# A second pair of up-projection columns by seven block products, and the last down-projection part in the common order of work

## The chip, the cores and the metric

One core of a Trainium2 chip runs the kernel as one launch. The metric is the device time of the launch in microseconds (us). Of the engines, PE is the matrix engine, DVE the vector engine, ACT the scalar engine, POOL and SP the two that here mainly issue DMAs. Each works through its own queue in order. Which instruction stands where in a queue was fixed when the program was compiled.

## The reference, cut to what matters

The whole is one step of a hybrid backbone for 128 context tokens and 512 latent tokens (640 in all, `D_MODEL` 1024). The change lies in its last stage, the gated MLP with a three-tap convolution along the tokens between the up-projection and the gate:

```python
def conv_ffn(h, w_up, conv_w, conv_b, w_down):
    L = h.shape[1]
    u = h @ w_up                       # (tokens, 1024) @ (1024, 2*2816)
    up = jnp.pad(u, ((0, 0), (1, 1), (0, 0)))
    uc = conv_w[0] * up[:, :L] + conv_w[1] * up[:, 1:L + 1] + conv_w[2] * up[:, 2:L + 2] + conv_b
    a, g = jnp.split(uc, 2, axis=-1)
    return (jax.nn.silu(g) * a) @ w_down
```

Its result is scaled, added to the residual and normalised. All matrices are float32. The kernel gets float32 products out of a faster matrix format by splitting each operand in a high part (rounded) and a low part (the rest), and by three matmuls for one: high by high, high by low, low by high.

## The kernel before, in words

**Tiles.** The 2816 hidden columns are 22 tiles of 128, taken in 11 pairs `p`. Pair `p` has an a half (`i` = 0) and a g half (`i` = 1), each 256 columns of `w_up`. The activations (`h2`, high and low) stand transposed, 128 features by tokens, 8 feature tiles, and tokens in two runs of `HW` = 322 columns.

**Two ways to multiply.** `plain_group` computes one half of a pair directly: four banks (two hidden tiles by two token runs) with 24 matmuls each, 96 in all. `unit_group` sees the same product as a product of 2 by 2 blocks and computes it by seven block products (`prod(m)`, in the order 1, 5, 6, 2, 3, 7, 4) with 12 matmuls each, 84 in all. For that it needs combinations of weight blocks, which `prep(m)` forms in place in the loaded tile and splits into high and low (DVE for four additions and five subtractions, ACT for copies, for m = 2 and 3 a DMA that accumulates), and combinations of activation blocks (`sa[1]` to `sa[4]`, high and low). Product 5 reads `sa[1]`, product 6 `sa[2]`, product 3 `sa[4]`, product 7 `sa[3]`. The results go to the pair's columns with a few additions on DVE and ACT.

**The sums of activations.** `diff` and `neg_sum` (L1174 to L1181) build the combinations in two scratch tiles on DVE, 128 by 1288 elements an operation; `hi_of` (L1188, ACT) and `lo_of` (L1191, DVE) split them. The fourth, in `last_sum`, is different: its high and low part overwrite the activation block `aq[1, 0]` itself, which `plain_group` reads. So `last_sum` is called inside the last bank of the plain g half.

**The order of work.** Pair 0 is computed ahead, while the last rows are still normalised. Then `groups` lists what follows: before the change pair 1's a half plain, `d0[0]`, pair 1's g half plain, `d0[1]`, then for each further pair two unit groups, with `down_groups` (the down-projection of finished pairs, four hidden tiles at a time) in between. `seq` is the list of all items of PE; the seventh product of a unit group is held back behind two items of the next group. `pump` traces loads and preparations as early as two `raw` tiles (1 MB each) and eight `wh` tiles allow. For PE the order written is the order run. DVE, ACT, POOL and SP get their order from a planner which, at each moment of a simulated run, takes the ready instruction that was traced first.

**The end before the change.** After the loop the last part of the down-projection (hidden tiles 18 to 21) stood alone: `load_w` loaded and split its weights, with DVE subtractions for the low parts, and `last_mm` ran tiles 18 and 19 for the first four row blocks, all column halves, which fills the time in which pair 10 passes convolution and gate. Then tiles 20 and 21 follow, `down_add`, `square` and `finish`.

The lines that fix the seven products' weights and activations are

```python
        PLAN = {1: ((0, 0), None), 5: ((0, 0), (0, 1)), 6: ((0, 0), (1, 1)), 2: ((1, 0), None),
                7: ((0, 1), (1, 1)), 4: ((0, 0), (1, 0)), 3: ((1, 1), None)}
        AOP = {1: aq[0, 0], 5: sa[1], 6: sa[2], 2: aq[0, 1], 7: sa[3], 4: aq[1, 1], 3: sa[4]}
```

Of the kernel before, what the change touches and what calls it, by code (L numbers as in the profile page):

```python
# [18 lines left out]
P = 128  # L19
DM = 1024  # L20
KD = DM // P
NT = 5
# [4 lines left out]
NF = FF // P  # L27
# [41 lines left out]
def hybrid_step(ctx: ExitStack, tc: tile.TileContext, a: dict, o: dict):  # L69
# [60 lines left out]
    def load_w(src, kk, n, lo_eng=None):  # L130
        return w_split(w_raw(src, kk, n), kk, n, lo_eng)

    def w_raw(src, kk, n):
        raw = wp([P, 4 * 512], F32, tag="raw", bufs=2)
        nc.sync.dma_start(raw[:, :kk * n].rearrange("p (k n) -> p k n", n=n), src.rearrange("(k p) n -> p k n", p=P))
        return raw

    def w_split(raw, kk, n, lo_eng=None):
        hs, ls = [], []
        step = 1024 // n  # L140
        for k0 in range(0, kk, step):
            w = min(step, kk - k0) * n
            rv = raw[:, k0 * n:k0 * n + w]
            hi = wp([P, 1024], F32R, tag="wh", bufs=8)[:, :w]
            lo = wp([P, 1024], F32R, tag="wh", bufs=8)[:, :w]
            nc.scalar.copy(hi, rv)  # L146
            if lo_eng == "dma":
                nc.scalar.activation(lo, rv, AF.Copy, scale=-1.0)
                nc.gpsimd.dma_start(lo, rv, accum_op=ALU.add)
            else:  # L150
                (lo_eng or V).tensor_sub(lo, rv, hi.bitcast(F32))  # L151
            for k in range(w // n):
                hs.append(hi[:, k * n:(k + 1) * n])
                ls.append(lo[:, k * n:(k + 1) * n])
        return hs, ls

    def mm3(ps, ah, al, bh, bl, start, stop):
        nc.tensor.matmul(ps, ah, bh, start=start, stop=False)  # L158
        nc.tensor.matmul(ps, ah, bl, start=False, stop=False)  # L159
        nc.tensor.matmul(ps, al, bh, start=False, stop=stop)  # L160
# [127 lines left out]
    mm = Pool("mm1", 5, space=PSUM)  # L288
# [233 lines left out]
    for i in (1, 0):  # L522
        ct, st = ctab[i], stab[i]
# [72 lines left out]
    mm = Pool("mm2", 1, space=PSUM)  # L596
# [129 lines left out]
    mm = Pool("mm3", 5, space=PSUM)  # L726
# [118 lines left out]
    st = states()  # L845
# [168 lines left out]
    def gt_pair():  # L1014
        return [gtp([P, 2, 2 * HW], F32R, tag=f"gt{i}", bufs=2) for i in range(2)]
# [7 lines left out]
    def x_row(dtype=F32):  # L1023
        return x1p([P, 768], dtype, tag="row", bufs=4)
# [3 lines left out]
    w_out, w_up, w_down = a["w_out"][0], a["w_up"][0], a["w_down"][0]  # L1028
# [40 lines left out]
    raw = w_raw(w_up[:, :256], 8, 256)  # L1069
# [6 lines left out]
    with tc.manual_schedule(engines={ET.PE}):  # L1076
        bank = {}
# [52 lines left out]
    def conv(f, i):  # L1130
        u, q = ub[f % 2][i], i * NF + f
        v = cvs[f, i] = x_row()[:, :641]
        nc.scalar.activation(v, u[:, 1:642], AF.Identity, scale=cw[:, 1, q:q + 1], bias=cw[:, 3, q:q + 1])
        V.scalar_tensor_tensor(v, u[:, 0:641], cw[:, 0, q:q + 1], v, op0=ALU.mult, op1=ALU.add)
        V.scalar_tensor_tensor(v, u[:, 2:643], cw[:, 2, q:q + 1], v, op0=ALU.mult, op1=ALU.add)
# [3 lines left out]
    def gate(f):  # L1139
        if f // 2 not in gts:  # L1140
            gts[f // 2] = gt_pair()
        r = [x[:, f % 2, :641] for x in gts[f // 2]]
        ca, cg = cvs[f, 0], cvs[f, 1]
        tg = t7([P, 641], tag="tg", bufs=1)
        nc.scalar.activation(tg, cg, AF.Tanh, scale=0.5)
        V.scalar_tensor_tensor(cg, tg, 1.0, cg, op0=ALU.add, op1=ALU.mult)
        V.tensor_mul(ca, ca, cg)
        nc.scalar.copy(r[0], ca)
        V.tensor_sub(r[1], ca, r[0].bitcast(F32))
# [17 lines left out]
    acc = Pool("acc7", 4, space=PSUM)  # L1167
    mm = Pool("mm7", 4, space=PSUM)
# [10 lines left out]
    def neg_sum(out, x, ys):  # L1179
        V.scalar_tensor_tensor(out, x, -1.0, ys[0], op0=ALU.mult, op1=ALU.subtract)  # L1180
        V.tensor_sub(out, out, ys[1])  # L1181
# [5 lines left out]
    def hi_of(m, x):  # L1187
        nc.scalar.copy(sa[m][0], x)  # L1188

    def lo_of(m, x):  # L1190
        V.tensor_sub(sa[m][1], x, sa[m][0].bitcast(F32))  # L1191
# [11 lines left out]
    def last_sum():  # L1203
        neg_sum(xs[0], xs[1], q[0, 1])
        hi_of(4, xs[0])
        lo_of(4, xs[0])
# [4 lines left out]
    def down_mm(ps, t, fs, w, part=None):  # L1211
        c0 = 0 if t == 0 else 129 + (t - 1) * P
        for n, f in enumerate(fs):
            if part is not None and n not in part:
                continue
            g = [x[:, f % 2, c0:c0 + P] for x in gts[f // 2]]
            mm3(ps, g[0], g[1], w[0][n], w[1][n], n == 0, n == len(fs) - 1)

    def down_add(ps, t, c0):
        n = ps.shape[1]  # L1220
        gs = slice(c0, c0 + n)
        tm = x_tmp()[:, :n]
        V.tensor_mul(tm, ps, gb[:, t == 0, gs])
        V.tensor_add(x1[:, t, gs], x1[:, t, gs], tm)  # L1224
# [32 lines left out]
    later = []  # L1257

    def plain_group(p, i):
        st = {}  # L1260

        def load():
            st["raw"] = w_raw(w_up[:, i * FF + 2 * p * P:i * FF + 2 * (p + 1) * P], 8, 256)

        def prep():
            st["w"] = w_split(st["raw"], 8, 256, "dma")

        def bank(f, h):
            def go():
                up_cols(f, i, st["w"], h * HW, (h + 1) * HW)  # L1270
                if h:
                    if i and f % 2:
                        last_sum()
                    later.append(lambda: conv(f, i))
                    if i and f % 2:
                        later.append(lambda: gate(f - 1))
                        later.append(lambda: gate(f))
            return go

        items = [bank(2 * p + f, h) for f in range(2) for h in range(2)]  # L1280
        return load, [(prep, 4, items)], items
# [74 lines left out]
    def down_groups(fs, step, after=()):  # L1356
        rows = slice(fs[0] * P, (fs[-1] + 1) * P)

        def group(g):
            st = {}  # L1360

            def load():
                st["raw"] = w_raw(w_down[rows, g * 512:(g + 1) * 512], len(fs), 512)

            def prep():
                st["w"] = w_split(st["raw"], len(fs), 512, "dma")

# [12 lines left out]

    d0 = down_groups([0, 1], 0)
    groups = [plain_group(1, 0), d0[0], plain_group(1, 1), d0[1]]
    for p in range(2, NF // 2):
        groups += [unit_group(p, 0), unit_group(p, 1)]
        if p % 2:
            d = down_groups(list(range(2 * p - 4, 2 * p)), 2 if p == 9 else 1, (2 * p + 1, 2 * p))
            groups = groups[:-1] + [d[0], groups[-1], d[1]]
    seq, held = [], []
    for _, _, items in groups:
        for x in items[:-1] if len(items) == 7 else items:  # L1390
# [34 lines left out]
    for fn in later:  # L1425
        fn()

    fs = list(range(NF - 4, NF))
    rows = slice(fs[0] * P, NF * P)
    ws = [load_w(w_down[rows, g * 512:(g + 1) * 512], 4, 512) for g in range(2)]  # L1430
    fg = wp([P, 4 * 512], F32, tag="raw", bufs=2)[:, :DM]
    nc.sync.dma_start(fg, a["final_g"].unsqueeze(0).to_broadcast([P, DM]))
    cols = {t: ((0, 512), (512, 256), (768, 256)) if t == NT - 1 else ((0, 512), (512, 512)) for t in range(NT)}
    bank = {}

    def last_mm(t, c0, n, part):
        if (t, c0) not in bank:
            pool, tag = ((acc, "acc"), (mm, "mm"))[t % 2]
            bank[t, c0] = pool([P, 512], tag=tag)[:, :n]
        g, cc = c0 // 512, slice(c0 % 512, c0 % 512 + n)  # L1440
        down_mm(bank[t, c0], t, fs, [[x[:, cc] for x in y] for y in ws[g]], part)

    with tc.manual_schedule(engines={ET.DVE, ET.PE}):
        for t in range(NT - 1):
            for c0, n in cols[t]:
                last_mm(t, c0, n, (0, 1))
        for t in range(NT):
            for c0, n in cols[t]:
                last_mm(t, c0, n, (2, 3) if t < NT - 1 else (0, 1, 2, 3))
                down_add(bank[t, c0], t, c0)  # L1450
                square(t, c0, n)
                if c0 == 0 and t == 3:
                    finish(0, 3)
        finish(NT - 2, 2)
# [37 lines left out]
```

## Time and profile before

| what | us |
| --- | --- |
| time, median of 3 runs (lowest to highest) | 1202.6 (1199.58 to 1203.64) |
| time of the profiled execution | 1202.29 |
| its span, first to last instruction | 1200.5 |
| PE busy in the span | 1160.6 |
| DVE busy | 736.5 |
| ACT busy | 567.1 |

The span is 1.8 us shorter than the time of the same execution; the rest lies before the first and after the last instruction. A row of the timeline gives the start and the length of an instruction in us, its engine, its line, its operation, the tile written and the tiles read, and in brackets how long the engine had been idle and who released it. A length includes the time that an instruction spends in the engine's pipeline, so consecutive starts show the rate better than lengths. In a row of the windows view, after the bounds, each engine's busy time stands with the number of its instructions, and behind the engines the granted clock of PE (1.00 is full), the busy share of the DMA engines and GB/s.

### The profile page before, as it was taken

To read this page: it belongs to the slowest core of one execution; us is meant where nothing else is said; L and a number is where in the kernel's file an instruction comes from. 1 tells how busy PE (TensorE), PEld (TensorE's weight loads), DVE (VectorE), ACT (ScalarE), POOL (GpSimd) and SP (SyncE) were. 2 spreads that over 40 slices of the span, in tenths; PEclk is the share of its full clock that TensorE was granted. 3 is DMA by queue.
4 is the path that set the end of the run, shared out by engine and by line. 5 is a ranking of instruction groups with operands and counts; after the bars stand their busy time and mean duration, and the time that the engine had idled before them with its cause. 6 is when DMAs were issued, how large, how long until landed. Compare 5 with 4: busy or idle time off the path is not lost.

```text
span 1200.5 us, 18330 instructions
## 1 busy us (share of the span) xinstructions
PE 1160.6 (97%) x7329; PEld 1043.8 (87%) x7329; DVE 736.5 (61%) x1428; ACT 567.1 (47%) x1013; POOL 173.9 (14%) x181
## 2 busy tenths in 40 slices
PE   4999999999999999999999999999999999999994
PEld 3788899999988888889999988999899898998884
DVE  5676977763234436453323259947677597677877
ACT  4345756551132324433322236667557465574453
POOL 0032200000012100042111122011111121122102
PEclk9999999999999999999999999999999999999998
DMA  8832111115564431112122459346657556677532
GB/s 283 273 113 71 36 36 36 36 59 166 198 215 148 141 97 44 36 36 70 39 92 82 158 126 184 89 113 116 139 140 170 131 105 133 128 136 171 120 96 87
DMA packets 129509, 139.54 MB, mean 116 GB/s; under 512 B 26240, under 2 KB 96976, under 8 KB 129424
## 3 DMA queue, kind: packets, MB, share of 16 engines
q1 hardware_dynamic: 104432, 109.01, 28.1%
q0 software_dynamic: 24272, 28.05, 14.4%
q8 instruction: 57, 0.93, 0.3%
q10 hardware_dynamic: 720, 1.31, 0.3%
q14 instruction: 28, 0.23, 0.1%
HBM read 110.31 MB, written 6.03 MB: 97 GB/s over the span
## 4 chain that ended last, share of the span: by engine, by line
PE 82%; DVE 8%; ACT 3%; issue 2%; DMA 2%; POOL 1%; SPq 0%; DVEq 0%; ACTq 0%; POOLq 0%
DMA weights.wh.379_10430<-weights.raw.369_10202 1%; DVE acts.u2.2_101 L1065 1%; DVE x1.u1.1_6381 L1224 1%; DMA xin.u1.1_112<-in_x_sample 0%; DMA weights.wh.394_10721<-weights.raw.382_10453 0%; DMA weights.raw.402_10915<-in_w_down 0%; POOL f0.s.5_3525 L901 0%; DVE acts.u1.1_100 L1064 0%; DVE x1.u1.1_6381 L1037 0%; DVE x1.u1.1_6381 L1254 0%; DVE gt.gt0.5_7260 L1175 0%; PE mm1.mm.11_318 L158 0%; PE mm7.mm.46_9644 L1327 0%; PE mm7.mm.34_8912 L1327 0%; PE mm7.mm.22_8180 L1327 0%
## 5 line engine op out<-in xcount | busy, mean ns | idle before, releaser
L790 POOL TENSOR_TENSOR ret.r2k.6_3635<-ret.u5.5_3528,ret.u1.1_3521 128x256 f32<-128x256 f32 x2 | 1.4, 740 | 205.0 <-ACT ret.u5.5_3528 L786 205.0
L1251 POOL TENSOR_TENSOR x1.u1.1_6381<-x1.u1.1_6381,weights.raw.407_10925 128x512 f32<-128x512 f32 x5 | 7.5, 1502 | 39.6 <-ACT x1.tm.112_10994 L1241 28.3
L839 DVE SCALAR_TENSOR_TENSOR ret2.u1.1_4322<-ret2.u1.1_4322,const.u14.14_94 64x128 f32<-64x128 f32 x24 | 6.8, 336 | 6.6 <-ACT ret2.u1.1_4322 L832 6.5
L1338 DVE TENSOR_TENSOR t7.u4.4_6930<-t7.u4.4_6930,const.u1.1_70 128x322 f32<-128x322 f32 x9 | 4.5, 496 | 10.1 <-ACT const.u1.1_70 L1337 10.1
L524 POOL TENSOR_TENSOR p1.u1.1_618<-p1.u3.3_622,p1q.u1.1_612 128x512 f32<-128x512 f32 x1 | 1.6, 1600 | 59.5 <-DMA p1.u4.4_624<-in_cache_k 59.5
L355 PE MATMUL mm1.mm.1_180<-const.u1.1_70,xin.u1.1_112 128*128 128x128 f32 x4 | 1.1, 434 | 9.3 <-DVE xin.u1.1_112 L348 9.3
L151 DVE TENSOR_TENSOR weights.wh.183_6570<-weights.raw.181_6567,weights.wh.182_6569 128x1024 fp32r<-128x1024 f32 x1 | 1.2, 1226 | 14.3 <-ACT weights.wh.182_6569 L146 14.3
L841 DVE SCALAR_TENSOR_TENSOR ret2.u1.1_4322<-ret2.u1.1_4322,const.u14.14_94 64x128 f32<-64x128 f32 x24 | 6.6, 382 | 4.8 <-ACT ret2.u1.1_4322 L834 4.8
L792 DVE TENSOR_TENSOR ret.u5.5_3528<-ret.u5.5_3528,ret.u1.1_3521 128x512 f32<-128x512 f32 x5 | 3.5, 693 | 9.4 <-POOL ret.r2k.8_3706 L790 3.3
L355 PEld LDWEIGHTS mm1.mm.1_180<-const.u1.1_70,xin.u1.1_112 128*128 128x128 f32 x4 | 0.7, 216 | 9.5 <-DVE xin.u1.1_112 L348 9.5
L392 ACT CAST acts.u1.1_100<-f0.s.1_113 128x640 fp32r<-128x640 f32 x4 | 2.9, 729 | 12.9 <-DVE f0.s.1_113 L390 12.9
L792 DVE TENSOR_TENSOR ret.u4.4_3527<-ret.u4.4_3527,ret.u1.1_3521 128x512 f32<-128x512 f32 x5 | 3.5, 692 | 9.0 <-POOL ret.r2k.11_3886 L790 4.7
L392 ACT CAST acts.u1.1_100<-f0.s.2_114 128x640 fp32r<-128x640 f32 x4 | 2.9, 730 | 9.9 <-DVE f0.s.2_114 L390 9.9
L151 DVE TENSOR_TENSOR weights.wh.108_4352<-weights.raw.106_4349,weights.wh.107_4351 128x1024 fp32r<-128x1024 f32 x1 | 1.2, 1226 | 10.3 <-ACT weights.wh.107_4351 L146 10.3
L901 POOL TENSOR_TENSOR f0.s.5_3525<-f0.s.5_3525,ret2.ny20.11_4904 128x512 f32<-128x512 f32 x5 | 6.0, 1238 | 9.1 <-DVE ret2.ny20.11_4904 L218 9.1
L146 ACT CAST weights.wh.112_4507<-weights.raw.111_4505 128x1024 fp32r<-128x1024 f32 x1 | 1.1, 1050 | 13.3 <-PE mm3.mm.36_4220 L159 13.3
L493 ACT ACTIVATE f0.s.3_724<-f0.s.3_724,p1q.ny20.11_892 128x128 f32<-128x128 f32 x20 | 6.0, 388 | 2.5 <-DVE p1q.ny20.11_892 L216 2.5
L828 POOL DMA_DIRECT2D out_new_state_ret_fwd<-ret.r2k.25_4345 x1 | 0.7, 662 | 43.8 <-ACT ret.r2k.25_4345 L827 43.8
L258 DVE COPY mod2.wr.9_4312<-aux3.aux.15_4279 128x128 f32<-128x128 f32 x1 | 0.3, 291 | 10.9 <-PE aux3.aux.15_4279 L255 10.9
L1235 DVE TENSOR_TENSOR x1.u1.1_6381<-x1.u1.1_6381,gate.u1.1_5311 128x512 f32<-128x512 f32 x10 | 6.7, 687 | 0.0
L1338 DVE TENSOR_TENSOR t7.u3.3_6929<-t7.u3.3_6929,const.u1.1_70 128x322 f32<-128x322 f32 x9 | 4.4, 494 | 3.4 <-ACT const.u1.1_70 L1337 3.4
L146 ACT CAST weights.wh.182_6569<-weights.raw.181_6567 128x1024 fp32r<-128x1024 f32 x1 | 1.1, 1055 | 11.5 <-PE mm3.mm.83_6401 L159 11.5
(7021 smaller groups left out, 4887.1 us busy)
## 6 DMA issues: line engine op xcount, KB each, us to landing
spill.u1.1_6389<-x1.u1.1_6381 POOLq DMA_DIRECT2D x5, 512.0 KB, 4.4
xin.u1.1_112<-in_x_sample SPq DMA_DIRECT2D x4, 512.0 KB
p0.u5.5_130<-in_w_mod SPq DMA_DIRECT2D x2, 1024.0 KB
p0.u6.6_135<-in_w_mod SPq DMA_DIRECT2D x2, 1024.0 KB
p0.u7.7_138<-in_w_mod SPq DMA_DIRECT2D x2, 1024.0 KB
mod.wm.2_2921<-in_w_mod SPq DMA_DIRECT2D x1, 2048.0 KB
mod.wm.4_3072<-in_w_mod SPq DMA_DIRECT2D x1, 2048.0 KB
mod.wm.6_3227<-in_w_mod SPq DMA_DIRECT2D x1, 2048.0 KB
```

What stands on the lines that cost most here:

```text
L151: (lo_eng or V).tensor_sub(lo, rv, hi.bitcast(F32))
L392: nc.scalar.copy(hT[0][:, k, :], xk)
L493: nc.scalar.activation(x[:, j], x[:, j], AF.Copy, scale=rstd[:, j:j + 1])
L792: V.tensor_mul(z, z, r1[:, t, 0:1, :].to_broadcast([P, 8, 64]))
L839: V.scalar_tensor_tensor(Ss[0:64, hh, st + 1, j], Ss[0:64, hh, st, j], cdsel[0:64, h:h + 1], Ss[0:64, hh, st + 1, j], op0=ALU.mult, op1=AL ...
L841: V.scalar_tensor_tensor(Ss[64:128, hh, 2 - st, j], Ss[64:128, hh, 3 - st, j], cdsel[64:128, h:h + 1], Ss[64:128, hh, 2 - st, j], op0=ALU. ...
L901: nc.gpsimd.tensor_mul(ov, ov, rso[:, 4 * t:4 * t + 4].unsqueeze(2).to_broadcast([P, 4, P]))
L1065: V.tensor_sub(d[1], hm, d[0].bitcast(F32))
L1224: V.tensor_add(x1[:, t, gs], x1[:, t, gs], tm)
L1235: V.tensor_mul(x1[:, t, gs], x1[:, t, gs], gb[:, t == 0, gs])
L1251: nc.gpsimd.tensor_mul(x1[:, t, lo], x1[:, t, lo], fg[:, lo])
L1338: V.tensor_sub(u[1][:, hi_u], u[1][:, hi_u], u3[i])
```

## The change

Pair 1 goes through `unit_group` for both halves; only pair 0 is plain. `last_sum` is called before the list of groups is built. The gates of pair 1 move behind the last item of `d0[1]`. The last part of the down-projection becomes two groups, `last_group(0)` and `last_group(1)`, at the end of `groups`: their items (tiles 18 and 19 of row blocks 0, 2, 1, 3) stand in `seq`, so the seventh product of pair 10 is held back behind two of them; their loads and preparations go through `pump`, and the low parts come from ACT and an accumulating DMA, as in the other down groups, and no longer from DVE. `plain_group` stays in the file, but nothing calls it.

```diff
-                    if i and f % 2:
+                    later.append(lambda: conv(f, i))
+                    if f % 2:
                         last_sum()
-                    later.append(lambda: conv(f, i))
-                    if i and f % 2:
-                        later.append(lambda: gate(f - 1))
-                        later.append(lambda: gate(f))
...
-    d0 = down_groups([0, 1], 0)
-    groups = [plain_group(1, 0), d0[0], plain_group(1, 1), d0[1]]
+    d0 = down_groups([0, 1], 0, (3, 2))
+    last_sum()
+    groups = [unit_group(1, 0), d0[0], unit_group(1, 1), d0[1]]
...
+    def last_group(g):
+        st = {}
+
+        def load():
+            st["raw"] = w_raw(w_down[fs[0] * P:, g * 512:(g + 1) * 512], 4, 512)
+
+        def prep():
+            ws[g] = w_split(st["raw"], 4, 512, "dma")
+
+        items = [lambda t=t: last_mm(t, g * 512, 512, (0, 1)) for t in (0, 2, 1, 3)]
+        return load, [(prep, 4, items)], items
+
+    groups += [last_group(0), last_group(1)]
...
-    ws = [load_w(w_down[rows, g * 512:(g + 1) * 512], 4, 512) for g in range(2)]
...
     with tc.manual_schedule(engines={ET.DVE, ET.PE}):
-        for t in range(NT - 1):
-            for c0, n in cols[t]:
-                last_mm(t, c0, n, (0, 1))
```

`last_mm`, `cols` and `bank` are moved up and not altered.

More of the change, by code (lines that the diff above doesn't have):

```diff
@@ L1387, in hybrid_step, with last_mm @@
             groups = groups[:-1] + [d[0], groups[-1], d[1]]
+    fs = list(range(NF - 4, NF))
+    cols = {t: ((0, 512), (512, 256), (768, 256)) if t == NT - 1 else ((0, 512), (512, 512)) for t in range(NT)}
+    bank, ws = {}, {}
+    def last_mm(t, c0, n, part):
+        if (t, c0) not in bank:
+            pool, tag = ((acc, "acc"), (mm, "mm"))[t % 2]
+            bank[t, c0] = pool([P, 512], tag=tag)[:, :n]
+        g, cc = c0 // 512, slice(c0 % 512, c0 % 512 + n)
+        down_mm(bank[t, c0], t, fs, [[x[:, cc] for x in y] for y in ws[g]], part)
+    def last_group(g):
[7 more added lines that the diff above has]
+    groups += [last_group(0), last_group(1)]
     seq, held = [], []
@@ L1426, in hybrid_step @@
         fn()
-    fs = list(range(NF - 4, NF))
-    rows = slice(fs[0] * P, NF * P)
-    ws = [load_w(w_down[rows, g * 512:(g + 1) * 512], 4, 512) for g in range(2)]
     fg = wp([P, 4 * 512], F32, tag="raw", bufs=2)[:, :DM]
     nc.sync.dma_start(fg, a["final_g"].unsqueeze(0).to_broadcast([P, DM]))
[L1433 to L1441, printed above, removed]
     with tc.manual_schedule(engines={ET.DVE, ET.PE}):
-        for t in range(NT - 1):
-            for c0, n in cols[t]:
-                last_mm(t, c0, n, (0, 1))
         for t in range(NT):
```

## The prediction

> **What bounds the kernel now.** I read the page first, for the shares, then the list of waits of PE, for what PE lacks, then the timelines and windows of the two places that the change touches.
>
> ```profile
> span 1200.5 us, 18330 instructions
> PE 1160.6 (97%) x7329; PEld 1043.8 (87%) x7329; DVE 736.5 (61%) x1428; ACT 567.1 (47%) x1013; POOL 173.9 (14%) x181
> ...
> PE mm7.mm.64_10766 L1324 <- ACT const.u1.1_70 L1337: 2.1, 1, 2.1
> PE aux3.aux.99_7057 L1053 <- DVE gt.gt0.1_6395 L1044: 0.9, 1, 0.9
> PE acc7.acc.46_10513 L159 <- DMA weights.wh.379_10430<-weights.raw.369_10202: 0.8, 1, 0.8
> ```
>
> PE works 97% of the span, and in the MLP its longest wait is 2.1 us. So matmuls taken away count in full, but only where PE still finds its operands ready. DVE's 61% is an average; what matters is DVE where the second pair begins:
>
> ```profile
> 749.30:769.40 20.10, 19.91 (x125) 19.71 (x123) 19.98 (x18) 12.98 (x17) 0.85 (x1) 1.00 0.32 85
> 769.40:780.00 10.60, 10.56 (x71) 10.56 (x72) 10.53 (x13) 6.27 (x10) 0.84 (x1) 1.00 0.44 106
> ...
> 780.00:785.00 5.00, 5.00 (x32) 4.82 (x32) 0.77 (x1) 3.29 (x5) 0.56 (x1) 1.00 0.01 3
> ```
>
> The third busy time is DVE's: 19.98 of 20.10 us and 10.53 of 10.60. For 30 us around the start of pair 1 (769.4) DVE has no free time; only behind 780 it has (0.77 of 5). PE is full there too, because plain products need nothing from DVE.
>
> **The change part by part.**
>
> *Matmuls saved.* From the windows of PE alone, one plain half and one small down group:
>
> ```profile
> 769.44:783.88 14.44, 14.44 (x97) 1.00 0.33 78
> 805.16:812.14 6.98, 6.98 (x33) 1.00 0.58 65
> ...
> 1146.02 0.31 PE L1324 MATMUL mm7.mm.66_10825<-acts.u1.1_100,weights.wh.393_10703 128*128 128x322 f32 x1
> 1147.82 0.31 PE L1324 MATMUL mm7.mm.65_10780<-acts.u1.1_100,weights.wh.394_10721 128*128 128x322 f32 x1
> ```
>
> 96 matmuls (the 97th belongs to the next item) take 14.44 us, 0.150 each; a block product of 12 takes 1147.82 - 1146.02 = 1.80 us. Two halves lose 2 x (96 - 84) = 24 matmuls: **-3.6 us**.
>
> *The new wait.* Plain products read only the activations. The unit group reads `sa[1]` second, `sa[2]` third and `sa[4]` fifth. PE reaches product 1 at 769.44 (row below) and product 3 four products later, 769.4 + 4 x 1.80 = **776.6**. When is `sa[4]` there?
>
> ```profile
> 745.82 1.05 DVE L1061 TENSOR_SCALAR x1.row.56_7074<-aux3.aux.100_7069,const.u8.8_88,const.u10.10_90 128x128 f32<-128x128 f32 x3 [1.19 <-PE aux3.aux.100_7069 L1053]
> 749.30 1.49 DVE L1175 TENSOR_TENSOR gt.gt0.5_7260<-acts.u1.1_100 128x1288 f32<-128x1288 f32 x1
> 755.32 0.88 DVE L1134 SCALAR_TENSOR_TENSOR x1.row.57_7212<-t7.u1.1_6927,t7.u5.5_6935,x1.row.57_7212 128x641 f32<-128x641 f32 x1
> 768.67 1.50 DVE L1191 TENSOR_TENSOR sums.u6.6_6923<-gt.gt0.5_7260,sums.u5.5_6922 128x1288 fp32r<-128x1288 f32 x1
> 770.08 0.89 DVE L1134 SCALAR_TENSOR_TENSOR x1.row.60_7224<-t7.u4.4_6930,t7.u5.5_6935,x1.row.60_7224 128x641 f32<-128x641 f32 x1
> 776.03 1.50 DVE L1181 TENSOR_TENSOR gt.gt0.5_7260<-gt.gt0.5_7260,acts.u2.2_101 128x1288 f32<-128x1288 f32 x1
> 777.44 0.83 DVE L1147 TENSOR_TENSOR x1.row.59_7220<-x1.row.59_7220,x1.row.60_7224 128x641 f32<-128x641 f32 x1
> ...
> 769.44 0.42 PE L1123 MATMUL mm7.mm.5_7315<-acts.u1.1_100,weights.wh.199_7296 128*128 128x322 f32 x1 [0.23 <-ACT gate.u1.1_5311 L275]
> ...
> 803.94 1.27 ACT L1188 CAST acts.u1.1_100<-gt.gt0.5_7260 128x1288 fp32r<-128x1288 f32 x1
> 805.41 1.49 DVE L1191 TENSOR_TENSOR acts.u2.2_101<-gt.gt0.5_7260,acts.u1.1_100 128x1288 fp32r<-128x1288 f32 x1
> ...
> 796.35 0.69 DVE L1310 TENSOR_TENSOR weights.wh.215_7486<-weights.raw.211_7433,weights.wh.215_7486 128x512 fp32r<-128x512 f32 x1 [7.32 <-ACT weights.wh.215_7486 L1305]
> 797.07 1.42 DVE L1302 TENSOR_TENSOR weights.raw.211_7433<-weights.raw.211_7433 128x512 f32<-128x512 f32 x2
> ```
>
> The difference behind `sa[4]` is already made early: its second step starts at 776.03 and the next DVE row at 777.44. Only its split waited for the plain half (803.94). After the change the split follows at once: 1.3 us ACT, 1.4 us DVE. This alone gives 780.2. But DVE also has to prepare the unit group's weights: a subtraction for product 1, an addition and a subtraction each for 5 and 6, again for 7 and 4, nine operations of 0.6 to 0.7 us. The plain half needed none; its low parts came by DMA. The scratch tile is reused (768.67 must end before the last sum may start), so the sums can't begin sooner, and the planner prefers them and pair 0's convolutions and gates, traced earlier.
>
> Five small operations, 5 x 0.61 = 3.1 us, must stand before product 6 has run; all nine are 5.5. The 1.2 us hole before 745.82 may take two of them. DVE can fill ACT's 1.3 us with the gate operations that stood behind 777.44. Early end: 780.2 + 3.1 - 1.2 - 1.3 = 780.8. Late end: 780.2 + 5.5 = 785.7, less a little where small operations fill bubbles, 785. I take the middle, **783.0**: planning by readiness lets the small ones slip between dependent sums, but not all of them. PE then stands 783.0 - 776.6 = 6.4 us (4.2 to 8.4). If instead the weights come late, product 5 or 6 stands and product 3 doesn't; the end is DVE's total either way.
>
> *The clock after a stall.*
>
> ```profile
> 1151.40 0.40 PE L158 MATMUL acc7.acc.51_10929<-weights.wh.398_10907,gt.gt0.25_10640 128*128 128x512 f32 x1
> 1154.38 0.51 PE L1324 MATMUL mm7.mm.64_10766<-acts.u1.1_100,weights.wh.396_10759 128*128 128x322 f32 x1 [2.12 <-ACT const.u1.1_70 L1337]
> 1157.64 0.55 PE L158 MATMUL acc7.acc.51_10929<-weights.wh.398_10907,gt.gt0.25_10640 128*128 128x512 f32 x1
> ...
> 1156.00:1157.00 1.00, 1.00 (x5) 1.00 (x5) 0.34 (x1) 0.63 (x1) 0.00 (x0) 0.50 0.00 0
> 1158.00:1159.00 1.00, 1.00 (x6) 0.80 (x5) 0.65 (x2) 0.97 (x2) 0.00 (x0) 1.00 0.00 0
> ```
>
> After 2.12 us of idling the granted clock is 0.50 until about 1158: the 12 matmuls take 3.26 us, not 1.80. So a stall of this length adds 1.5 us, and I add **1.6** for the longer one. The Trainium skill, "TensorE: Matmul & The Clock Gate", section "HAM oscillation — how this bites in real kernels", says that idle gaps beyond about 3.4 us bring this on; here 2.12 us did, so the measurement decides. Head: 6.4 + 1.6 - 3.6 = **+4.4 us** (4.2 + 1.5 - 3.6 = +2.1 to 8.4 + 1.7 - 3.6 = +6.5).
>
> *What is hidden.* The weights of the g half and of `d0`: DVE has room again behind 780, and product 4 and five down items (1.8 + 7.0 = 8.8 us) lie ahead of the g half.
>
> ```profile
> 751.91 0.37 SPq L135 DMA_DIRECT2D weights.raw.203_7306<-in_w_up  x1
> ```
>
> The load of the g half went out at 751.91, when the first `raw` tile was free. That tile is now freed some 33 us later (785), as its additions are in place; SP then loads the g half into the tile of `d0[0]`. If that cover fails, a 1 MB load (5 us, below) shows. The moved gates of pair 1 are needed only by pair 3's down group and by pair 2's convolution buffers, six products (10.8 us) later. All at nothing.
>
> *The last part.* Before, PE waits for ACT, whose queue is held by a load:
>
> ```profile
> 1147.70 0.37 SPq L135 DMA_DIRECT2D weights.raw.402_10915<-in_w_down  x1
> 1144.99 1.06 ACT L146 CAST weights.wh.398_10907<-weights.raw.397_10905 128x1024 fp32r<-128x1024 f32 x1
> 1152.95 1.04 ACT L146 CAST weights.wh.403_10917<-weights.raw.402_10915 128x1024 fp32r<-128x1024 f32 x1 [4.80 <-DMA weights.raw.402_10915<-in_w_down]
> 1153.90 0.42 ACT L1337 COPY const.u1.1_70<-mm7.mm.64_10766 128x322 f32<-128x322 f32 x1
> ...
> 1166.77 0.83 DVE L1149 TENSOR_TENSOR gt.gt1.28_10892<-x1.row.108_10808,gt.gt0.27_10891 128x641 fp32r<-128x641 f32 x1 [0.80 <-ACT gt.gt0.27_10891 L1148]
> 1168.27 0.39 PE L158 MATMUL acc7.acc.51_10929<-weights.wh.400_10911,gt.gt0.27_10891 128*128 128x512 f32 x1
> ...
> weights.wh.205_7309<-weights.raw.198_7294 POOLq DMA_DIRECT2D x1, 512.0 KB, 4.5
> weights.wh.379_10430<-weights.raw.369_10202 POOLq DMA_DIRECT2D x1, 512.0 KB, 7.8
> ```
>
> Tiles 20 and 21 begin at 1168.27, as eight items and the gates (1167.6) are done. After the change two items (12 matmuls, 2.8 us) stand ahead of the held product and would cover the wait of 2.1 and its 1.5 of slow clock: at best -3.4. But the `raw` tile for this load is freed no sooner, and the low parts now come from an accumulating DMA: 4.5 us alone, 7.8 beside a load. ACT's copy of the first tile can't be much before 1145 (it stood at 1144.99), its negated one then ends by 1147, so the low part lands between 1152 and 1155; PE wants it at 1151.6, behind its first matmul of 1151.40. The load of 1147.70 is slowed by the same transfers, and ACT's L1337 still stands behind it. I take a stall of about the old size at another place, and 0.5 us for the DVE subtraction that no longer lies among the gates: **-0.5** (-3.4 to +2.0). If the accumulate lands in 4.5 us and L1337 is planned ahead of the load, -3.4; if it takes 7.8 and the copy waits for the load, +2.
>
> *Sum*, against the execution of 1202.3 (span 1200.5 and 1.8 around it; the median is 1202.6): 1202.3 + 4.4 - 0.5 = **1206.2**.
>
> **The rivals.**
>
> 1. *The stall is at its short end and the tail gains.* Small operations fill every bubble of DVE: +2.1, and -3.4 at the end: 1201.0. For it: 1.2 us of hole and many dependent pairs on DVE. Against it: the 7.8 us row.
> 2. *No stall at the head: faster.* The mechanism is the place of the last sum. If the planner puts it and the weights ahead of pair 0's gates and convolutions (8 of them, 0.8 us each, between 755.32 and 772), the low part of `sa[4]` is done by 776.6, PE never waits, and the saving of 3.6 stands, with the tail 1195.3 to 1198.7. It decides at 776.6. Against it: before, the last sum's first step could start at 770.1 and stood third or fourth behind such operations.
> 3. *The tail turns worse.* The accumulate lands at 1155, PE idles 3.4 us, runs at half clock, and the held product waits for ACT until 1158: +2 and +4.4 and, with the late end of the head, 1209 to 1211.
> 4. *The tail's stall costs no clock.* The half clock may come only with longer stalls than the tail's 2 us. PE's tail is then 1.5 us shorter: 1204.7. Against it stands the 0.50 row after 2.12 us. The rule of the page above, in the Trainium skill, would give this.
>
> **How the numbers follow.** The forecast has 0.48, rival 1 0.22, rival 2 0.08, rival 3 0.12, rival 4 0.10. The range runs from 1200.5 to 1210.5 and leaves out rival 2 and the far ends of rivals 1 and 3; the forecast's own range is 1203.5 to 1208.5. A measurement of this kernel can tell some 0.3% (3.6 us) from no change, so slower means above 1206.2, where the forecast itself stands, and faster below 1199.0. Slower: half of the forecast and the share of it with late weights (0.30), rival 3 (0.12), a little of rival 4: 0.43. Faster: rival 2 and the lowest end of rival 1, 0.10. The rest, 0.47, is no change that can be told. So the sign is forecast, a loss, and its size lies at the edge of what can be seen.
>
> **What would show it.** Right: a wait of PE of 4 to 8 us in the fifth product of pair 1 (L1324 or L1326) on the DVE row L1191 that writes `acts`, half clock behind it; the first product of pair 2 at 814 to 819 instead of 812.14 (812.1 is the end of the last `d0` window). At the end a wait on a `wh` DMA or on L1337. Wrong: no wait of PE in pair 1, or a wait for a `raw` load, or tiles 20 and 21 starting by more than 3 us earlier, seen from the last seventh product.

## The result, and the profile after

The changed kernel takes 1215.62 us (median of 5 runs, 1214.95 to 1217.9) against 1201.42 before (1199.46 to 1203.64): a ratio of 1.0124, 95% interval 1.0107 to 1.0142. It is slower by 14 us. The forecast had the sign, 1206.2 us, and the time lies 5 us above the upper end of its range, 1210.5.

Two lines of the page after the change, and of the list of PE's waits those from the end of the normalisation on (engine, first tile and line, what it waited for, total, times, longest):

```profile
span 1213.8 us, 18334 instructions
...
PE 1161.2 (96%) x7305; PEld 1042.4 (86%) x7305; DVE 743.5 (61%) x1454; ACT 571.9 (47%) x1029; POOL 178.6 (15%) x185
```

```profile
...
PE acc7.acc.53_10978 L159 <- DMA weights.wh.410_10937<-weights.raw.407_10838: 5.3, 1, 5.3
PE mm7.mm.6_7350 L1321 <- ACT acts.u1.1_100 L1188: 3.8, 1, 3.8
...
PE aux3.aux.99_7057 L1053 <- DVE gt.gt0.1_6395 L1044: 2.0, 1, 2.0
PE mm7.mm.6_7350 L1323 <- DVE acts.u2.2_101 L1191: 1.9, 1, 1.9
PE acc7.acc.53_10978 L158 <- ACT weights.wh.409_10936 L146: 1.7, 1, 1.7
PE mm7.mm.11_7702 L1321 <- ACT t7.u1.1_6927 L1326: 1.3, 1, 1.3
```

24 matmuls are gone, as counted. But the busy time of PE is not shorter, because some matmuls ran at half clock, and the waits are longer: 3.8 and 1.9 us for the last sum (L1188 is its high part, L1191 its low part), 1.7 and 5.3 us for the second tile of the last w_down part. Before, the longest in the MLP was 2.1. (In the changed file the seven products' matmuls stand at L1321, L1323 and L1324, their weights' additions at L1299, copies at L1302, subtractions at L1307.)

Four rows of PE's timeline cut the run into stretches: the first product of pair 1, the first of pair 2, the first item of the last w_down part, and the start of its tiles 20 and 21.

```profile
770.41 0.42 PE L1321 MATMUL mm7.mm.5_7330<-acts.u1.1_100,weights.wh.199_7300 128*128 128x322 f32 x1
...
818.08 0.31 PE L1321 MATMUL mm7.mm.11_7702<-acts.u1.1_100,weights.wh.221_7546 128*128 128x322 f32 x1
...
1159.37 0.40 PE L158 MATMUL acc7.acc.51_10908<-weights.wh.403_10828,gt.gt0.25_10662 128*128 128x512 f32 x1
...
1181.63 0.39 PE L158 MATMUL acc7.acc.51_10908<-weights.wh.405_10833,gt.gt0.27_10957 128*128 128x512 f32 x1
```

| stretch, us | before | after | difference |
| --- | --- | --- | --- |
| to the first product of pair 1 | 769.44 | 770.41 | +0.97 |
| from there to pair 2 ("head") | 42.70 | 47.67 | +4.97 |
| pair 2 to the last part | 339.26 | 341.29 | +2.03 |
| last part to tiles 20/21 ("tail") | 16.87 | 22.26 | +5.39 |
| tiles 20/21 to the end | 32.23 | 32.17 | -0.06 |
| span | 1200.5 | 1213.8 | +13.3 |

(The ends of before are the rows 769.44, 1151.40 and 1168.27 and the window's end 812.14 in the prediction.) The loss has two places of its own, and two small ones.

**The head** on ACT, DVE and PE:

```profile
775.53 1.49 DVE L1180 SCALAR_TENSOR_TENSOR gt.gt0.5_7260<-gt.gt1.6_7261,acts.u1.1_100 128x1288 f32<-128x1288 f32 x1
...
778.41 1.49 DVE L1181 TENSOR_TENSOR gt.gt0.5_7260<-gt.gt0.5_7260,acts.u2.2_101 128x1288 f32<-128x1288 f32 x1
779.08 0.62 ACT L1302 CAST weights.wh.210_7364<-weights.raw.207_7328 128x512 fp32r<-128x512 f32 x1 [2.58 <-DMA weights.raw.207_7328<-in_w_up]
780.24 1.26 ACT L1188 CAST acts.u1.1_100<-gt.gt0.5_7260 128x1288 fp32r<-128x1288 f32 x1
781.11 0.69 DVE L1307 TENSOR_TENSOR weights.wh.204_7320<-weights.raw.197_7296,weights.wh.204_7320 128x512 fp32r<-128x512 f32 x1
781.71 0.69 DVE L1307 TENSOR_TENSOR weights.wh.208_7345<-weights.raw.197_7296,weights.wh.208_7345 128x512 fp32r<-128x512 f32 x1
782.31 1.50 DVE L1191 TENSOR_TENSOR acts.u2.2_101<-gt.gt0.5_7260,acts.u1.1_100 128x1288 fp32r<-128x1288 f32 x1
...
783.86 0.64 PE L1323 MATMUL mm7.mm.6_7350<-acts.u2.2_101,weights.wh.203_7315 128*128 128x322 f32 x1 [1.90 <-DVE acts.u2.2_101 L1191]
```

The low part of the last sum runs from 782.31 to 783.8 (forecast: ready at 783.0), and PE stands 3.75 us for the high part and 1.90 for the low part, 5.65 us in all (forecast 6.4). What was larger is the slow clock behind it (windows of 2 us; the granted clock is the number behind the engines):

```profile
782.00:784.00 2.00, 0.14 (x1) 0.14 (x1) 2.00 (x3) 0.00 (x0) 0.00 (x0) 0.59 0.25 29
784.00:786.00 2.00, 2.00 (x8) 2.00 (x9) 1.97 (x4) 0.56 (x1) 0.00 (x0) 0.50 0.64 234
786.00:788.00 2.00, 2.00 (x9) 2.00 (x8) 0.92 (x3) 0.06 (x1) 0.00 (x0) 0.50 0.00 0
788.00:790.00 2.00, 2.00 (x11) 1.95 (x10) 1.01 (x3) 0.04 (x1) 0.00 (x0) 0.70 0.00 0
```

0.59 and 0.70 are means: half clock from 782.4 (1.64 of the first 2 us) to 789.2 (1.2 of the last). From 783.86 on PE works in it, 5.3 us that yield half: 2.7 lost. 42.70 - 3.6 + 5.65 + 2.7 = 47.45 of 47.67.

**The tail.** SP's waits, SP's and PE's rows, and the transfer (the DMA view gives KB and us from issue to landing):

```profile
SPq L135 <- DMA weights.wh.206_7324<-weights.raw.198_7298: 33.7, 1, 33.7
...
SPq L135 <- DMA weights.wh.406_10834<-weights.raw.398_10688: 15.8, 1, 15.8
```

```profile
1162.12 0.37 SPq L135 DMA_DIRECT2D weights.raw.407_10838<-in_w_down  x1
...
1174.40 0.80 PE L159 MATMUL acc7.acc.53_10978<-weights.wh.410_10937,gt.gt0.25_10662 128*128 128x512 f32 x1 [5.29 <-DMA weights.wh.410_10937<-weights.raw.407_10838]
```

```profile
weights.wh.406_10834<-weights.raw.398_10688 POOLq DMA_DIRECT2D x1, 512.0 KB, 5.4
```

The stall that stood at the held product (2.1 us) is gone, as two items now stand ahead of it. But the load of the second tile goes out at 1162.12; before it went out at 1147.70. SP waits 15.8 us for the accumulating DMA that makes the first tile's low part, since that DMA is the last reader of the `raw` tile which the load needs. (The row above it is the same wait in the head: the g half's load, raw.207, behind the accumulate of `d0[0]`.) PE is through with the first tile and product 4 at 1166.9 and waits 1.7 us for the second tile's high part and 5.3 for its low part.

### The profile page after: what moved, and what is told of

It is laid out like the page before. It is cut to its first block, busy times and chain, and to the rows that moved or that the text cites. A ratio compares the mean times of both kernels' runs of the same rounds, so it can differ in the third digit from the quotient of the medians.

```text
span 1213.8 us, 18334 instructions
## 1 busy us (share of the span) xinstructions
PE 1161.2 (96%) x7305; PEld 1042.4 (86%) x7305; DVE 743.5 (61%) x1454; ACT 571.9 (47%) x1029; POOL 178.6 (15%) x185
## 3 DMA queue, kind: packets, MB, share of 16 engines
q0 software_dynamic: 26384, 29.10, 15.1%
## 4 chain that ended last, share of the span: by engine, by line
PE 75%; DVE 10%; DMA 5%; ACT 4%; issue 4%; POOL 1%; SPq 0%; DVEq 0%; POOLq 0%; ACTq 0%
DMA t7.u5.5_6935<-in_conv_w 1%; DMA weights.raw.344_9704<-in_w_up 1%; DMA weights.raw.386_10456<-in_w_up 1%; DVE x1.u1.1_6381 L1224 1%; POOL x1.u1.1_6381 L1037 1%; DMA weights.wh.406_10834<-weights.raw.398_10688 0%; DMA xin.u1.1_112<-in_x_sample 0%; DMA weights.raw.407_10838<-in_w_down 0%; DMA weights.raw.398_10688<-in_w_down 0%; DMA weights.raw.207_7328<-in_w_up 0%; POOL f0.s.5_3525 L901 0%; DMA weights.wh.410_10937<-weights.raw.407_10838 0%; DVE x1.u1.1_6381 L1231 0%; DVE acts.u2.2_101 L1065 0%; DMA x1.u1.1_6381<-in_x_prompt 0%
## 5 line engine op out<-in xcount | busy, mean ns | idle before, releaser
L146 ACT CAST weights.wh.112_4507<-weights.raw.111_4505 128x1024 fp32r<-128x1024 f32 x1 | 1.1, 1050 | 13.3 <-PE mm3.mm.36_4220 L159 13.3
```

## The experiments

T is my theory after this reading: two separate losses that add, in the head by the late last sum, in the tail by the late second load. Its rivals: R1, the head is the whole loss and the tail's wait only follows; R2, the tail's loss is the accumulating DMAs, whenever the load starts; R3, a unit half in pair 1 costs by its preparations wherever it stands; R4, the loss sits in the tail alone. In what follows "head" and "tail" are the stretches of the table.

**e1 and e2: each part alone.** e1 has the new lines around `last_sum()` and `groups` with the old end, e2 the old beginning with the two `last_group` lines.

> The new beginning of the second pair, with the last w_down part as before. T (two separate losses that add): about +8 us over before (1209 to 1210), PE waiting 5 to 6.5 us for the split of the last sum in product 3 of pair 1, the first product of pair 2 at 817 to 819, and tiles 20/21 8 us later than 1168.27. R1 (the head is the whole loss, the tail's wait only follows from it): +13 to +14, 1215. R4 (the loss sits in the tail, the head's is caught up later): +0 to +4.

> The old plain halves, with only the last w_down part in the common sequence. T: about +5 us (1206 to 1208), PE waiting 4 to 8 us for the second of the two last loads, which goes out behind the end of the last seventh product, at about 1154. R1: within 1 us of before. R4: +10 or more.

e1: 1208.83 us, ratio 1.0063 (1.0039 to 1.0088); PE waits 3.6 and 1.9 for the last sum, head 47.46. e2: 1208.76 us, ratio 1.0063 (1.0047 to 1.0079); waits of 1.9 and 5.3, tail 23.43, the load at 1155.51, 3 us behind the last seventh product (1152.48). 6.8 + 6.7 = 13.5 us against 14.2 together: within the intervals the two losses add. R1 and R4 fall. e2 is 0.8 us above the upper end that I gave it; e1 is 0.2 to 1.2 us better than I expected, for which the last section has a reason.

**e3: the held product's weights prepared first.** In `preps.sort` product 4 of pair 10 comes ahead of the first last tile:

```diff
-    preps.sort(key=lambda z: z[4])
+    preps.sort(key=lambda z: z[4] - 2.5 * (z[0] == len(groups) - 3 and z[4] > pos[id(groups[-2][2][0])]))
```

> The changed kernel, only the preparation of the held product 4 of the last pair sorted ahead of the four tiles of the first last load, so that its raw tile comes free for the second load. T (the late start of the load is the tail's loss): the load goes out about 10 us earlier than 1162.12, the wait of 5.3 goes, tail 5 to 8 us shorter, 1207 to 1211. R2 (the accumulating DMAs are the loss, whenever the load starts): the wait of about 5 us stays, 1214 to 1216.

1213.91 us, ratio 1.0105 (1.009 to 1.0121): above T's range and just under R2's. The second load goes out at 1156.69, 5.4 us sooner (I had expected 10), and PE no longer waits for the second tile. But another has come, for the first tile:

```profile
PE acc7.acc.51_10908 L159 <- DMA weights.wh.406_10852<-weights.raw.398_10688: 3.8, 1, 3.8
```

```profile
weights.wh.406_10852<-weights.raw.398_10688 POOLq DMA_DIRECT2D x1, 512.0 KB, 7.1
```

The first tile's accumulate now starts later (POOL at 1157.60, after the change 1154.68), and it runs beside the load: 7.1 us, after the change 4.6. The tail is 18.56 us, 3.7 shorter than after the change; in the profiled execution 1.5 us of this are lost again ahead of pair 1, which the edit doesn't touch (half clock, last section). So T as I had put it was half of it: where the load comes early, the accumulate is late, and where the accumulate is early, the load waits for it.

**e4: one half plain.** e3's tail; pair 1 as `[plain_group(1, 0), d0[0], unit_group(1, 1), d0[1]]`, `last_sum()` in the plain half's last bank.

> The first output half of pair 1 plain again, the second by seven products, and the tail of the run before this one: 12 matmuls (1.8 us) fewer than before. T: no wait of PE in pair 1, because the last sum is split beside the small w_down group that stands between the halves; pair 2 begins at 810 to 811; with a tail as good as before's 1199 to 1200, with the tail's cover 1196 to 1198. R3 (a unit half in pair 1 costs by its preparations on DVE wherever it stands): a wait of 2 us or more in the second half, 1202 to 1205.

1203.42 us, ratio 1.0016 (1.0006 to 1.0026). PE waits nowhere in pair 1, head 40.87, that is 42.70 - 1.83: the 12 matmuls. R3's wait on DVE doesn't come. The end of the normalisation, too, is as before (0.9 instead of 2.0 us on L1044). Two of my numbers missed: the tail has e3's accumulate again (3.5 us), and in pair 2 PE waits 1.3 us for ACT, as it does after the change: a unit half's preparations do cost something, on ACT and one pair later.

**e5 and e6: the low parts of the last tiles by DVE.** One word is taken out, in e4 (which gives e5) and in the changed kernel (e6):

```diff
-            ws[g] = w_split(st["raw"], 4, 512, "dma")
+            ws[g] = w_split(st["raw"], 4, 512)
```

> The kernel of e4 (first output half of pair 1 plain, product 4 prepared first), with the low parts of the two last w_down tiles subtracted on DVE instead of accumulated by a DMA. T, as e3 and e4 left it (an accumulating DMA that runs beside the next load takes 7 us instead of 4.6, and PE waits 3.5 us for it): no wait of PE at the end, about 5 us less than e4's 1203.4 (3.5 of wait, 1.5 of half clock): 1197 to 1199, below before. Rival (the load itself is late, in whatever way the low part is made): a wait of 2 us or more moves to the high part or to the subtraction, 1201 to 1204.

> The changed kernel, with only the low parts of the two last w_down tiles subtracted on DVE; the order of the preparations as in the change. Raw tile theory (the second load waits until the first tile is read, and the accumulate is its last reader): the tile is free some 4 us sooner, the load goes out at 1157 to 1159 instead of 1162.12 and is split by 1166, the waits of 1.7 and 5.3 go: 1207 to 1210. Rival (the load waits for product 4's preparation and the wh tiles, whoever reads the raw tile last): the load still goes out behind 1161, the wait shrinks only by the accumulate's 4.5 us less the 1 us of a subtraction: 1211 to 1213.

e6: 1208.59 us, ratio 1.0054 (1.0039 to 1.0069), 7.0 us less than the changed kernel, by one word. SP's waits and rows:

```profile
SPq L135 <- DVE weights.wh.406_10833 L151: 6.2, 1, 6.2
```

```profile
1156.55 0.37 SPq L135 DMA_DIRECT2D weights.raw.407_10836<-in_w_down  x1
```

The last reader of the raw tile is now a DVE subtraction of 1.2 us, the load goes out 5.6 us sooner, and in the tail PE waits for nothing: 12.96 us, 9.3 less than after the change and 3.9 less than before. With the waits of 6.99 us and 1.96 for the half clock behind them (1174.40 to 1178.32, which yields half) this gives 21.91 of the changed kernel's 22.26.

The raw tile theory holds, and the accumulating DMA is its reason. But e6 changes two things at once: the tile is free sooner, and the second tile's own low part takes 1.2 us on DVE instead of 4.5 by DMA. No run splits them. An estimate from the rows after the change: the second tile's low part was there at 1174.4, PE wanted it at 1167.1; the load alone, 5.6 us sooner, would still leave 1.7 us of the 7.0. So the late load is the larger share, and R2, which blamed the accumulates wherever the load stands, is right for the smaller one.

e5: 1200.0 us, ratio 0.9984 (0.9974 to 0.9995), the first below before, but 1 us over the expectation. PE waits 1.5 us for the gates of the last pair, and ACT's rows show why:

```profile
1151.69 1.05 ACT L146 CAST weights.wh.406_10923<-weights.raw.401_10775 128x1024 fp32r<-128x1024 f32 x1 [4.55 <-DMA weights.raw.401_10775<-in_w_down]
1152.64 0.42 ACT L1334 COPY const.u1.1_70<-mm7.mm.63_10781 128x322 f32<-128x322 f32 x1
...
1160.96 0.73 ACT L1148 CAST gt.gt0.27_10942<-x1.row.107_10777 128x641 fp32r<-128x641 f32 x1 [1.69 <-DVE x1.row.107_10777 L1147]
```

Here the load comes so early that ACT's copy of it stands, waiting, ahead of the copy of product 7 (PE was done with it at 1150.4), and the convolution and gates follow late. It is the same hold-up on ACT that before had in its tail. In e6 the load lands after product 7's copy and holds nobody.

**e7 and e8: what makes the last sum late?** Both change e1. In e7 `last_sum()` is called ahead of the two gates of pair 0; in e8 pair 1's first half makes all its low parts by DMA: `if m in (2, 3) or (p, i) == (1, 0):`.

> The kernel of e1 (only the new beginning), with the last sum traced ahead of pair 0's two gates. T (the last sum stands behind convolutions and gates on DVE): its two steps come 3 us earlier, PE's wait in product 3 shrinks from 5.5 to 1.5 to 3 us, 1204 to 1206 against e1's 1208.8. Rival (the weights' small operations or ACT's copies hold it): the wait stays within 1 us, 1207.5 to 1209.

> The kernel of e1, with all seven low parts of pair 1's first half made by ACT and an accumulating DMA: five subtractions of 0.6 us fewer on DVE, three of them out of the end of the normalisation, two from ahead of the last sum's split. T: product 1 starts 0.5 us earlier, the wait in product 3 is 1 to 1.5 us shorter: 1206 to 1207.5. Rival (the weights' share is nothing, gates and sums alone set the end): no change, 1208.5 to 1209. Against both: if DMA or ACT can't deliver the low part of product 1, 5 or 6 in time, PE waits there and it is slower than e1.

e7: 1207.08 us, ratio 1.0043 (1.0028 to 1.0058), its runs from 1202.46 to 1210.22, so against e1 only the head is read: 45.12, 2.3 us less. Of these, 1.3 are the waits, 3.0 and 1.1 instead of 3.6 and 1.9, and the rest is the clock, half for 3.4 us instead of 6.8. Counted from the first product of pair 1, PE has the whole sum 1.3 us sooner (784.10 - 772.15 = 11.95, in e1 783.42 - 770.13 = 13.29). By the times of the span it isn't sooner: this execution came to pair 1 2.0 us later than e1's, for a reason ahead of it (half clock behind L1053, last section). T gave 2.5 to 4 us; what holds the sum now, the rows show:

```profile
778.68 1.49 DVE L1181 TENSOR_TENSOR gt.gt0.5_7260<-gt.gt0.5_7260,acts.u2.2_101 128x1288 f32<-128x1288 f32 x1
...
780.73 0.62 ACT L1303 CAST weights.wh.210_7364<-weights.raw.207_7328 128x512 fp32r<-128x512 f32 x1 [2.47 <-DMA weights.raw.207_7328<-in_w_up]
781.25 1.26 ACT L1188 CAST acts.u1.1_100<-gt.gt0.5_7260 128x1288 fp32r<-128x1288 f32 x1
```

DVE is done with the sum at 780.1 (1.4 us after 778.68), and ACT stands until 780.73 on a load, that of the g half's weights; the high part follows behind it. So gates, subtractions and this load all stand near the end of the same chain.

e8: 1216.66 us, ratio 1.0121 (1.0104 to 1.0138), 8 us slower than e1, against both theories. DVE's row:

```profile
745.05 0.69 DVE L1299 TENSOR_TENSOR weights.raw.197_7296<-weights.raw.197_7296 128x512 f32<-128x512 f32 x1 [4.16 <-DMA weights.wh.199_7300<-weights.raw.197_7296]
```

The additions write into the loaded tile, so the first of them must now wait until product 1's accumulate has read it. It stands in DVE's queue ahead of the normalisation (L1044), and PE waits there 5.4 us instead of 2.0. Of the 9.6 us by which its span is longer than e1's, 6.2 lie ahead of pair 1 (the wait and half clock behind it), 1.0 in the head and 2.2 in the tail. I had counted operations of DVE and not asked what they would wait for. The share of the five subtractions isn't measured by this.

**e9 to e12: what can be had.** e9 is e6's tail with e4's beginning. e12 is e6's tail with the beginning as before. e10 is e6 with e7's order and product 7 ahead of product 3 in pair 1's first half. There the convolution of that half's second block follows product 7 and so leaves product 3 out of its lower half: e10 doesn't compute the MLP and counts for its times alone. e11 puts the convolution behind product 3. The lines in which e10 differs from e6 (without the old call of `last_sum()`, which goes):

```diff
+    last_sum()
     for f in range(2):
         gate(f)
...
-        order = (1, 5, 6, 2, 3, 7, 4)
+        order = (1, 5, 6, 2, 7, 3, 4) if (p, i) == (1, 0) else (1, 5, 6, 2, 3, 7, 4)
```

> The tail of e6 (order of the change, low parts of the last two w_down tiles by DVE) with the beginning of e4 (first output half of pair 1 plain, second by seven products). T (the losses and gains of the two places add, and the load placed late leaves ACT free for product 7's copy): e6's tail, from the end of the last seventh product to the start of tiles 20/21 13 us against 16.9 before, and pair 2 at 810: 1196.5 to 1198.5, 2 to 3 below e5's 1200.0. Rival (tail gains don't add, since the gates of the last pair then end last): 1199.5 to 1201.

> The changed kernel with e6's tail, the last sum traced ahead of pair 0's gates (e7), and in the first half of pair 1 product 7 ahead of product 3, so that PE has 1.8 us more to do before it needs the last sum. T: PE's wait in pair 1 falls from 5.65 to about 2.3 us and its slow clock to 1.5 to 2, the rest of the head's loss (1.0 from the normalisation, 0.5 to 1.3 from ACT in pair 2) stays: 1199 to 1203, no loss against before but no better than e9. Rival (product 7's low part comes as late as the last sum, so that only the place of the wait changes): 1204 to 1207.

> The kernel of e10, with the convolution of pair 1's second block put behind product 3 again (in e10 it followed product 7 and so read the lower half of that block without product 3). T: the convolution moves by one product and nothing waits for it before pair 3, so the time of e10 stays: 1200 to 1204, within 0.3% of before. Rival (the convolution's place on ACT and DVE matters here): 1.5 us or more to either side of e10's 1202.9.

> The beginning as before (both halves of pair 1 plain), and only the tail of e6: last w_down part in the common sequence, its low parts by DVE. T: the tail alone gains 3.9 us less what the gates take back: 1197.5 to 1199.5; e9 is at most 1 us better, since its 12 saved matmuls (1.8 us) are followed by ACT's 1.3 us wait in pair 2. Rival (the tail's gain came with the new beginning): 1201 to 1203.

| kernel | us | ratio to before (95%) | head | pair 2 to last part | tail |
| --- | --- | --- | --- | --- | --- |
| e9 | 1198.02 | 0.9968 (0.9956 to 0.998) | 40.88 | 341.47 | 13.26 |
| e10 | 1202.92 | 1.0007 (0.9997 to 1.0017) | 42.26 | 341.31 | 12.96 |
| e11 | 1201.88 | 0.9998 (0.999 to 1.0007) | 42.23 | 341.23 | 12.95 |
| e12 | 1198.68 | 0.9966 (0.9954 to 0.9979) | 42.69 | 339.22 | 13.00 |

e12 and e9 are 3.4 and 3.6 us below before, further below the changed kernel, and can't be told apart: e9's 1.8 us of saved matmuls in the head come back behind pair 2 (341.47 against 339.22). So the tail alone holds all of the gain, and it is the 3.9 us that e6 showed. In e10 and e11 PE's two waits in pair 1 are 1.7 and 0.8 us and the clock stays full, so the head is 0.5 us shorter than before's; the third stretch is 2 us longer. With both places mended the seven products for both halves end level with before and 3.2 us behind e12.

## Why the prediction was right or wrong

**Matmuls: right.** -3.6 for two halves; e4 measured -1.83 for one.

**The wait for the last sum: right in the main.** 5.65 us against 6.4, at the product and for the tile named. The first product of pair 2 stood at 818.08, forecast 814 to 819. That the difference fits so well is in part luck: both its ends came some 1 us later than forecast, PE at product 3 at 777.8 instead of 776.6 and the low part at 783.8 instead of 783.0. And the larger part of the wait, 3.75 us, ended with the high part on ACT (L1188); the DVE row that I named ended only the last 1.90. e7 confirms 1.3 us of the reason given (planned behind pair 0's gates), and adds one that I had costed at nothing, the g half's load on ACT's queue.

**The clock behind it: under-sized.** +1.6 was the price of the one slow stretch in the trace of before. After 5.65 us of idling two such stretches followed, 2.7 us. In e7, after waits of 3.0 and 1.1, it was one.

**"All at nothing": wrong, by 2 to 3 us.** The small operations that "may take" the 1.2 us hole before 745.82 do so at a price. DVE before the change, then after it:

```profile
743.88 0.75 DVE L1044 TENSOR_SCALAR gt.gt0.1_6395<-x1.u1.1_6381,x1.ny1.51_6899 128x1024 f32<-128x1024 f32 x1
```

```profile
743.34 0.69 DVE L1307 TENSOR_TENSOR weights.wh.200_7304<-weights.raw.197_7296,weights.wh.200_7304 128x512 fp32r<-128x512 f32 x1
...
744.47 0.69 DVE L1299 TENSOR_TENSOR weights.raw.197_7296<-weights.raw.197_7296 128x512 f32<-128x512 f32 x1
745.07 0.75 DVE L1044 TENSOR_SCALAR gt.gt0.1_6395<-x1.u1.1_6381,x1.ny1.51_6899 128x1024 f32<-128x1024 f32 x1
```

Product 1's subtraction and the first addition stand in DVE's queue ahead of the normalisation's L1044, which starts 1.2 us later, and PE's wait there grows from 0.9 to 2.0 us. e4, e5 and e9, without them, have 0.9 again.

In the third stretch PE waits 1.3 us for ACT's copy of pair 2's product 1 (0.5 to 1.3 us in every run whose second half is a unit group, nothing in those with two plain halves). The rows suggest why: the g half's tile is freed late, pair 2's load into it goes out at 802.65 instead of 789.10, and the preparations then pile up on ACT ahead of that copy. No run moves this load alone, so the reason is argued and not shown. The rest of the +2.0 is busy time of PE (337.8 us instead of 337.0 for as many matmuls), for which the runs show no reason. I had named as cover of the g half's load product 4 and five down items, and they did cover the load; they didn't cover what comes after it.

**The tail: wrong, and the largest error.** The step that failed is "I take a stall of about the old size at another place", -0.5 us; it was +5.4. The sentence ahead of it holds the cause: "the `raw` tile for this load is freed no sooner, and the low parts now come from an accumulating DMA". Both halves were right, and I didn't put them together: an accumulating DMA of 4.6 to 5.4 us is then the last reader of that tile, and the load waits for it. I followed the first tile's low part to PE (it came in time: POOL at 1154.68 and 4.6 us, PE wants it at 1159.6) and not the second tile's load to its release. The lower bound, -3.4 (its parts, 2.1 and 1.5, add up to 3.6), was the true worth of the two items ahead of the held product; e6 and e12 have it with -3.9, e9 with -3.6.

**Rivals.** Rival 1's tail gain and rival 3's late accumulate were both real mechanisms, in e6 and e3, but in other kernels than the one forecast. Rival 2 fell at the head (5.65 us). Rival 4, a stall of about 2 us at the end that costs no clock, was not put to the test by the change, whose waits there were 1.7 and 5.3 us; e1 and e7 show that it can happen. No rival had a late second load.

## What to carry to other kernels

For each load that a change moves, ask what frees its buffer, and follow that releaser's full length: a reader that is a DMA of 5 us holds a buffer 4 us longer than a subtraction of 1.2 us, and it is slower still beside a load (7.1 us in e3). Ask of each small operation that fills a bubble what stands behind it in its queue. Where a change makes PE wait, price the clock too: in these runs nothing or 1.5 us behind a wait of 2 us, and one to three stretches of half clock, 3.41 us each, behind longer ones. When a change has two parts, run each alone with its cheapest repair before the whole is judged; here a third of a per cent lay in one of them.

## What the runs showed of the hardware

**Half clock comes in stretches of one length, and their starts lie on a grid.** Between 700 and 1184 us of the span every stretch of half clock lasted 3.41 us, or two times that (6.83) or three times (10.24, e2). Where an execution has several, their starts lie whole lengths of 3.413 us apart: after the change 782.37 and 1171.49 (114 lengths), in e7 746.13 and 783.68 (11), in e8 747.26, 788.22 and 1170.51 (12 and 124). So this grid runs on by itself, and a wait doesn't set it. The Trainium skill, "TensorE: Matmul & The Clock Gate", section "Part 1: The HAM clock gate (the "warmup" mystery)", speaks of a free-running activity window of some 3.4 us; the lengths and the starts agree with it.

**So the same wait can cost 1.5 us or nothing.** At L1053 the changed kernel and e3 run the same code and PE waits as long. Its rows and the windows behind, after the change and in e3:

```profile
745.88 0.66 PE L1053 MATMUL aux3.aux.99_7057<-const.u1.1_70,gt.gt0.1_6395 128*128 128x128 f32 x4 [1.99 <-DVE gt.gt0.1_6395 L1044]
...
746.00:748.00 2.00, 2.00 (x19) 2.00 (x19) 2.00 (x6) 2.00 (x6) 0.83 (x1) 1.00 0.00 0
```

```profile
745.80 1.03 PE L1053 MATMUL aux3.aux.99_7057<-const.u1.1_70,gt.gt0.1_6395 128*128 128x128 f32 x4 [2.00 <-DVE gt.gt0.1_6395 L1044]
...
746.00:748.00 2.00, 2.00 (x11) 2.00 (x11) 1.22 (x3) 1.86 (x6) 0.92 (x1) 0.50 0.00 0
```

The difference is where the wait lies on the grid, carried on from each execution's slow stretches. In e3 it fell into one length as a whole; after the change the end of one length, at 744.82, cut it in 0.93 and 1.06. All PE waits of the nine runs with a slow stretch sort this way: with the clock full, 1.99 us or more of idling within one length was followed by half clock, 1.44 or less was not, and nothing lies between. (With the clock half, even 0.94 us kept it there, in e2.) These are readings of this kernel's traces and no more.

The wait at the end, for product 7's copy, is the same case: 2.12 us before, all within one length; 2.39 in e8, 2.12 of them within one; 1.77 in e1 and 1.88 in e7, both cut by the end of a length, with at most 1.30 and 1.37 within one. Windows of 1 us behind it, e1 and e8:

```profile
1161.00:1162.00 1.00, 0.79 (x5) 0.79 (x6) 1.00 (x1) 1.00 (x2) 0.00 (x0) 1.00 0.00 0
1162.00:1163.00 1.00, 1.00 (x9) 1.00 (x8) 0.56 (x4) 0.57 (x2) 0.00 (x0) 1.00 0.00 0
1163.00:1164.00 1.00, 1.00 (x6) 0.86 (x5) 0.50 (x1) 0.97 (x3) 0.00 (x0) 1.00 0.00 0
```

```profile
1170.00:1171.00 1.00, 1.00 (x7) 1.00 (x6) 0.57 (x4) 0.57 (x2) 0.00 (x0) 0.76 0.00 0
1171.00:1172.00 1.00, 1.00 (x5) 0.90 (x5) 0.50 (x1) 0.67 (x2) 0.00 (x0) 0.50 0.00 0
1172.00:1173.00 1.00, 1.00 (x4) 0.81 (x3) 1.00 (x3) 0.97 (x2) 0.00 (x0) 0.50 0.00 0
1173.00:1174.00 1.00, 1.00 (x4) 0.81 (x3) 1.00 (x2) 0.18 (x1) 0.00 (x0) 0.54 0.00 0
```

e1 and e7 keep the full clock; their tails are 15.0 and 15.1 us, before's 16.87 and e8's 17.15. So in e1's profiled execution (1207.54 us) the tail was 1.9 us better than before's, 0.35 by the wait and the rest by the clock, which is why e1 came out better than expected there. Of its other executions two took 1210 us at a mean granted clock of 0.988 and one 1205.94 at 0.993, against 0.991 here. That fits more and fewer such stretches; no trace shows these executions.
